# In segment 3 all transposes to tokens on VectorE; other places for mLSTM's chunks and for segment 0's inverse products

## The chip, the cores and the metric

One core of one Trainium2 chip. The metric is the device time of one execution in microseconds; lower is better. Engines are named as the profile names them: PE is TensorE (matmuls and transposes against an identity), DVE is VectorE, ACT is ScalarE, POOL is GpSimd, SP issues DMAs.

## What is computed

A decoder layer for 2048 tokens of width 1024 in float32. One input projection feeds two groups of heads: 4 heads of an mLSTM (key 128, value 256) and 8 heads of a gated DeltaNet (GDN; key and value 128). Both run in chunks with a state carried from chunk to chunk; one output projection follows. Of the reference, what matters here:

```python
# mLSTM, per chunk
num = (w_inter[..., None] * jnp.einsum('bhld,bhde->bhle', qi, C)
       + jnp.einsum('bhls,bhse->bhle', P, vi))
C = decay[..., None, None] * C + jnp.einsum('bhs,bhsd,bhse->bhde', ws, ki, vi)
...
# GDN: the inverse of a unit lower triangular matrix, then the chain of chunks
a_mat = lower + jnp.eye(CHUNK, dtype=lower.dtype)
sol = lax.linalg.triangular_solve(a_mat, rhs, left_side=True, lower=True, unit_diagonal=True)
...
v_new = Ui - jnp.einsum('bhld,bhde->bhle', Wi, S)
S = (jnp.exp(g_last)[..., None, None] * S
     + jnp.einsum('bhld,bhle->bhde', ki * jnp.exp(g_last[..., None] - gi)[..., None], v_new))
```

## The kernel before

The tokens are cut into 4 segments of 512, each with 4 chunks of 128. A segment is a row of windows: P0 M0 P1 M1 P2 M2 P3 M3, in the last segment P0 M0 P1 M1 P2 P3 M2 M3. A P window projects q, k, v and the gate of one pair of GDN heads (with a short convolution on DVE, L703 and L709); an M window projects one mLSTM head. The projection's matmuls fill the window, and `window()` (L1026) mixes other work between them, the streams: each stream is a generator, and a list of places (shares of the window's length, or a start, an end and a number of even steps between them) says when it makes its next step. The code is run on PE in the order in which it is written (`manual_schedule` for PE); the order of the instructions on DVE, ACT, POOL and SP is set by a scheduler when the kernel is built, with priorities as hints. Each engine executes its own list strictly in order.

Names are built as kind, segment, pair or head, chunk: `vr3_1_3` belongs to segment 3, pair 1, chunk 3. The streams, and the names that the prediction uses:

- `g_prep` of a pair: its k, q and v become "token-major" (`ktok`, `gv`), products of keys `kk` on PE, `ua` from them on DVE (L835), and then the **substitution**: 62 small DVE operations in a strict chain, 31 times L853 and L857 on `xb`/`tb`, with the columns shrinking from 31 blocks of 8 to 1. Its result goes to DRAM and back (`e_d`, L859; `E`, L863, four DMAs that SP issues).
- `g_level` of a pair: three DVE transposes turn `E` into `dmz` (L907, L908, L907), and four products on PE combine the small inverses: `zp` (L913), `fp` (L922), `zq` (L933), `fq` (L939). Between zp and fp ACT copies `dmz` from PSUM (L917), between fp and zq ACT writes `E` (L926) and DVE transposes it (L928).
- `g_chain` of a pair: four chunks, each `vp` (the transposes of v, when PE does them, L957), `sp`, `vr` on DVE (L979), `vq` (L985), a copy on ACT, `su`, `op`, the states `SS` on DVE (L1009), and the gated output `gyt` (L1021).
- `m_chunks` of a head: four chunks, each `nd` and `up` (L620, or L623 to L625 in split form), then on DVE the state `CN` (L651, L653) and the output `yt` (L670). In segment 0 the keys are weighted into `kws` by ACT (L612) and DVE (L613), four pieces in turn.

A block of 128x128 can be turned to tokens in two ways, by table, for each segment class (first, middle, last) and each pair or head: by PE against an identity (L957 for v, L773 for k, L876 for q, L602 for mLSTM's k), four instructions for 128x512; or by DVE, sixteen instructions of 32x128 (L504, in `to_tokens`), and for q by a reduction that transposes (L871, L888, L890). `VT`, `KTR`, `QT`, `MT` are the tables. In the middle segments (1 and 2) all of it is on DVE already. For q, k and v of a pair, an entry 1 means DVE.

After segment 3 comes a tail with the output projection, 16 tiles.

Of the kernel before, what the change touches and what calls it, by code (L numbers as in the profile page):

```python
# [26 lines left out]
XKB = 2  # L27
PRI = 400

LVP = (0.26, 0.3, 0.34, 0.4, 0.45)  # L30


CHP = (0.42, 0.46, 0.63, 0.71, 0.88)
CHM = (0.03, 0.11, 0.28, 0.45, 0.53, 0.7, 0.87, 0.95)
MW, MPR, VPR = ((0.07, 0.85), 200, 200)
MCP = (0.6, 0.75, 0.875)
MC2 = (0.0, 0.1, 0.18, 0.25, 0.32)
RMSP = (0.2, 0.22, 0.55, 0.55)
# [14 lines left out]
GN = 2  # L53


VT = ((0, 0, 0, 0), (1, 1, 1, 1), (1, 0, 0, 0))
KTR = ((0, 0, 0, 0), (1, 1, 1, 1), (0, 1, 0, 0))
QT = ((1, 1, 1, 1), (1, 1, 1, 1), (1, 1, 0, 1))
MT = ((0, 0, 0, 0), (1, 1, 1, 1), (1, 1, 1, 0))
KF = ((0, 1, 1, 1), (1, 1, 1, 1), (1, 1, 1, 0))  # L60
MF = ((1, 1, 1, 0), (1, 1, 1, 0), (1, 0, 0, 0))
KE = ('vector', 'gpsimd')
# [7 lines left out]
def hybrid_layer(  # L70
# [872 lines left out]
    def g_chain(seg, pr, r, st):  # L943
# [7 lines left out]
        def tok(c):  # L951
            n_ = f"{s_}_{c}"
            vr = sm.tile([P, 2, P], F32, tag="vr", name=f"vr{n_}", bufs=2)
            if not by_dve(VT, seg, pr):
                vp = psc.tile([P, 512], F32, tag="cp", name=f"vp{n_}")
# [146 lines left out]
    lvl, chain, mch = {}, {}, {}  # L1102
    st = None
    for seg in range(NSEG):
        last = seg == NSEG - 1
        pst, st = st, {}
        if seg:
            with tc.high_priority(PRI):
                build_h(pst["xks"])
        raw[0] = seg == 0  # L1110
        gs = gate_steps(seg, st)

        def nextrms():
            yield
            d = rms_stats(seg + 1)
            yield
            rbc = wkp.tile([P, T], F32, tag="gbc", name=f"rbc{seg + 1}", bufs=2)
            rms_bcast(seg + 1, d, rbc)
            yield
            st["xks"] = load_h(seg + 1, rbc)  # L1120

        for kind, n in ORDER_LAST if last else ORDER:
            r = {}
            streams, keep = [], ()
            if kind == "P":
                q = 3 if n == 0 else n - 1
                if n == 0 and seg:
                    streams.append((mch.pop(3), MC2, None, None, 2 * PRI))
                if n == 0:
                    streams.append((gs, GP, None, None, PRI))  # L1130
                    if seg == 0:
                        streams.append((rms_first_bcast(), (RB,), None, None, PRI))
                if last and n == 3:
                    streams.append((prep2, 10, 0.0, 0.2, PRI))
                    if LVB[0] < 0:
                        streams.append((lvl[2], NLV, 1 + LVB[0], 1 + LVB[1], PRI))
                elif last and n == 2:
                    streams += [(lvl[q], LVA[0], None, None, PRI), (chain[q], NCS, LVA[1], LVA[2], PRI),
                                (mch[q], 8, MW[0], MW[1], MPR)]
                elif q in chain:  # L1140
                    streams += [(lvl[q], LVP, None, None, PRI), (chain[q], CHP, None, None, PRI)]
                    if q in mch:
                        streams.append((mch[q], 8, MW[0], MW[1], MPR))
                    keep = (chain[q],)
                window(g_proj(seg, n, r, st), WIN, streams, keep)
                lvl[n], chain[n] = g_level(seg, n, r), g_chain(seg, n, r, st)
                prep = g_prep(seg, n, r, st)
                if last and n == 2:
                    prep2 = prep
            else:  # L1150
                if last and n == 2:
                    if LVB[0] >= 0:
                        streams.append((lvl[2], NLV, LVB[0], LVB[1], PRI))
                    streams += [(prep, 10, 0.0, 0.25, PRI), (chain[2], NCS, LVB[2], LVB[3], PRI)]
                    if LVC[0] < 0:
                        streams.append((lvl[3], NLV, 1 + LVC[0], 1 + LVC[1], PRI))
                elif last and n == 3:
                    if LVC[0] >= 0:
                        streams.append((lvl[3], NLV, LVC[0], LVC[1], PRI))
                    streams += [(mch[2], 8, LVC[4], LVC[5], PRI),  # L1160
                                (chain[3], NCS, LVC[2], LVC[3], PRI)]
                else:
                    streams.append((prep, 10, 0.0, 0.25, PRI))
                    if (n - 1) % 4 in chain:
                        streams.append((chain[(n - 1) % 4], CHM, None, None, PRI))
                mch[n] = m_chunks(seg, n, r, st)
                if n == 3:
                    if last:
                        streams.append((wout_early(), WOP, None, None, 0))
                    else:  # L1170
                        streams.append((nextrms(), RMSP, None, None, 0))
                    streams.append((mch[n], MCL if last else MCP, None, None, 0))
                    keep = (mch[n],)
                window(m_proj(seg, n, r), WIN, streams, keep)
# [232 lines left out]
```

## Time and profile before

| what | value |
|---|---|
| time, median of 3 runs | 2287.14 us (2284.95 to 2287.39) |
| the profiled execution | 2287.61 us |
| its span | 2285.8 us, 41796 instructions |
| granted PE clock, mean | 0.988 |
| busy PE, DVE, ACT, POOL | 2204.7, 1829.0, 861.3, 804.4 us |
| segment 0 (first to last window) | 7 to 485 us |
| segments 1, 2 and 3 | 485 to 956, 956 to 1420, 1420 to 1905 us |
| tail | 1905 to 2286 us |

The profile gives for one execution the busy time of each engine, what ended its idle time (a wait is put down to the instruction that came last), and a timeline of instructions. Granted clock 1.00 is 2.4 GHz and 0.50 is 1.2 GHz. Times inside the profile count from the span's start; 1.8 us of the profiled execution lie around the span.

### The profile page before, as it was taken

The page shows a single profiled execution, that of the slowest core. Times are in us where ns is not written, and L with a number is a line of the kernel's source. Part 1 is how long each engine was busy: PE and PEld are TensorE (multiplying, and loading weights), DVE is VectorE, ACT ScalarE, POOL GpSimd, SP SyncE. Part 2 cuts the span into 40 slices and gives each one's busy share as a digit, 9 for nine tenths or more (in the row PEclk, how much of TensorE's full clock was granted, in tenths as well). Part 3 has the DMA queues.
Part 4 walks back from the last instruction along what each step waited for, and adds up shares of the span by engine and source line. Part 5 has one row for each costly group of instructions (what it writes and reads, how often), then busy time and mean ns, then how long its engine had stood idle before and what let it go on. Part 6 is the DMA issues. An engine that isn't in the chain of part 4 may idle for free.

```text
span 2285.8 us, 41796 instructions
## 1 busy us (share of the span) xinstructions
PE 2204.7 (96%) x14814; PEld 1956.3 (86%) x14814; DVE 1829.0 (80%) x5108; ACT 861.3 (38%) x2289; POOL 804.4 (35%) x1219
## 2 busy tenths in 40 slices
PE   8989999989999999999999999999999999999998
PEld 7869898987989898978898989798988997788777
DVE  8978878778997979889979798698767737878784
ACT  5535454535343434352424243434244334111111
POOL 5747565652121202521212124212111115555543
PEclk9999999999999999999999999999999999999999
DMA  8767767764636364655454547454546544222321
GB/s 288 265 213 243 246 225 244 263 223 138 213 129 210 138 218 150 233 167 182 158 192 160 187 162 239 154 172 167 183 166 208 188 158 162 80 97 91 102 83 65
DMA packets 183322, 409.19 MB, mean 179 GB/s; under 512 B 51736, under 2 KB 84632, under 8 KB 183112
## 3 DMA queue, kind: packets, MB, share of 16 engines
q1 hardware_dynamic: 182392, 405.74, 52.4%
q8 instruction: 116, 1.90, 0.3%
q14 instruction: 94, 0.77, 0.1%
q10 hardware_dynamic: 720, 0.79, 0.1%
HBM read 309.68 MB, written 96.90 MB: 178 GB/s over the span
## 4 chain that ended last, share of the span: by engine, by line
PE 53%; DVE 27%; POOL 4%; DMA 4%; issue 4%; ACT 3%; SPq 0%; POOLq 0%; ACTq 0%; DVEq 0%
DVE ytt L1222 5%; DVE ktok L504 3%; PE pt_gz L365 2%; PE pt_gz L363 2%; PE pt_gz L364 2%; PE po L1263 2%; PE po L1262 2%; PE po L1261 2%; DVE gv L504 2%; PE pt_mv L363 2%; PE pt_mo L365 2%; PE pt_mo L363 2%; PE pt_mo L364 2%; PE pt_mv L365 2%; PE pt_mv L364 2%
## 5 line engine op out<-in xcount | busy, mean ns | idle before, releaser
L1222 DVE STREAM_TRANSPOSE ytt<-yl 32x256 f32<-32x256 f32 x448 | 195.3, 436 | 45.3 <-POOL ylo L1190 39.2
L1019 POOL TENSOR_TENSOR gms<-gms,nhalf 128x2 f32<-128x2 f32 x64 | 49.8, 779 | 401.2 <-DVE gms L1017 400.9
L853 DVE TENSOR_TENSOR tb<-xb,lbt 128x248 f32<-128x248 f32 (+30 forms) x496 | 167.1, 337 | 28.8 <-DMA lbt<-l_d 16.2
L857 DVE TENSOR_TENSOR xb<-xb,tb 128x248 f32<-128x248 f32 (+30 forms) x496 | 167.6, 338 | 13.1
L363 PE MATMUL pt_gz<-whi_P,hh 128*128 128x256 f32 (+1 forms) x512 | 151.2, 295 | 4.8 <-ACT hh L341 3.4
L365 PE MATMUL pt_gz<-whi_P,hl 128*128 128x256 f32 (+1 forms) x512 | 147.6, 288 | 2.4 <-DVE hl L342 2.4
L364 PE MATMUL pt_gz<-wlo_P,hh 128*128 128x256 f32 (+1 forms) x512 | 147.6, 288 | 1.8 <-DVE wlo_P L182 1.8
L363 PE MATMUL pt_mo<-whi_M,hh 128*128 128x256 f32 x512 | 148.3, 290 | 0.0
L363 PE MATMUL pt_mz<-whi_M,hh 128*128 128x256 f32 x512 | 147.7, 288 | 0.0
L363 PE MATMUL pt_mv<-whi_M,hh 128*128 128x256 f32 x512 | 147.0, 287 | 0.0
L365 PE MATMUL pt_mo<-whi_M,hl 128*128 128x256 f32 x512 | 144.2, 282 | 0.0
L365 PE MATMUL pt_mz<-whi_M,hl 128*128 128x256 f32 x512 | 144.1, 281 | 0.0
L364 PE MATMUL pt_mv<-wlo_M,hh 128*128 128x256 f32 x512 | 144.1, 281 | 0.0
L365 PE MATMUL pt_mv<-whi_M,hl 128*128 128x256 f32 x512 | 144.0, 281 | 0.0
L364 PE MATMUL pt_mo<-wlo_M,hh 128*128 128x256 f32 x512 | 144.0, 281 | 0.0
L364 PE MATMUL pt_mz<-wlo_M,hh 128*128 128x256 f32 x512 | 144.0, 281 | 0.0
L1270 ACT ACTIVATE jkf<-xr 128x512 f32<-128x512 f32 (+1 forms) x33 | 20.4, 619 | 271.8 <-DVE xr L1268 148.1
L1261 PE MATMUL po<-woh,yh 128*128 128x512 f32 (+1 forms) x297 | 114.6, 386 | 1.7 <-ACT yh L1188 1.7
L1262 PE MATMUL po<-wol,yh 128*128 128x512 f32 (+1 forms) x297 | 114.4, 385 | 0.9 <-POOL wol L1068 0.9
L1263 PE MATMUL po<-woh,ylo 128*128 128x512 f32 (+1 forms) x297 | 114.7, 386 | 0.1
L182 POOL TENSOR_TENSOR wlo_M<-wraw_M,whi_M 128x256 fp32r<-128x256 f32 x128 | 99.8, 811 | 40.5 <-ACT whi_M L179 40.2
L182 POOL TENSOR_TENSOR wlo_P<-wraw_P,whi_P 128x256 fp32r<-128x256 f32 x104 | 87.9, 874 | 62.9 <-ACT whi_P L179 58.1
(409 smaller groups left out, 7543.5 us busy)
## 6 DMA issues: line engine op xcount, KB each, us to landing
whi_M<-wdM SPq DMA_DIRECT2D x96, 512.0 KB, 3.8
wlo_M<-wdM SPq DMA_DIRECT2D x96, 512.0 KB, 5.1
whi_P<-wdP SPq DMA_DIRECT2D x90, 512.0 KB, 4.1
wlo_P<-wdP SPq DMA_DIRECT2D x90, 512.0 KB, 5.6
wraw_M<-in_wg_dram SPq DMA_DIRECT2D x32, 512.0 KB, 6.6
wdM<-whi_M SPq DMA_DIRECT2D x32, 512.0 KB, 2.7
wdM<-wlo_M SPq DMA_DIRECT2D x32, 512.0 KB, 3.0
wraw_P<-in_wg_dram SPq DMA_DIRECT2D x30, 512.0 KB, 7.2
```

The source lines that it names most:

```text
L182: eng.tensor_tensor(lo[:, ks, :], raw_[:, ks, :], hi[:, ks, :].bitcast(F32), op=ALU.subtract)
L363: nc.tensor.matmul(ps, lhsT=hh[k][:, ts], rhs=hi, start=(k == 0), stop=False)
L364: nc.tensor.matmul(ps, lhsT=hh[k][:, ts], rhs=lo, start=False, stop=False)
L365: nc.tensor.matmul(ps, lhsT=hl[k][:, ts], rhs=hi, start=False, stop=(k == KT - 1))
L504: nc.vector.transpose(dst[32 * a:32 * a + 32, :, 32 * b:32 * b + 32], s4[32 * b:32 * b + 32, :, a, :])
L853: nc.vector.tensor_tensor(tb[:, :, 0:n], xb[:, :, i:i + 1].broadcast_to([P, 8, n]), lbt[:, i:i + 1, i + 1:32].broadcast_to([P, 8, n]), op= ...
L857: nc.vector.tensor_tensor(xs, xs, tb[:, :, 0:n], op=ALU.subtract)
L1019: nc.gpsimd.tensor_tensor(ms, ms, nhalf[:, 0:2], op=ALU.pow)
L1222: nc.vector.transpose(ytt[32 * b:32 * b + 32, :, 32 * a:32 * a + 32], y3[32 * a:32 * a + 32, :, 32 * b:32 * b + 32])
L1261: nc.tensor.matmul(ps, lhsT=yh, rhs=woh, start=(k == 0), stop=False)
L1262: nc.tensor.matmul(ps, lhsT=yh, rhs=wol, start=False, stop=False)
L1263: nc.tensor.matmul(ps, lhsT=ylo, rhs=woh, start=False, stop=(k == 15))
```

## The change

Three edits. The last row of the four tables becomes all 1: in segment 3 every transpose to tokens is on DVE. `MW`, a start and an end for eight even places (two steps a chunk, so 0.07, 0.181, 0.293, 0.404, 0.516, 0.627, 0.739, 0.85), becomes a written list of eight. In segment 0 the inverse products of a pair get the places `LV0` in the next pair's window.

```diff
-LVP = (0.26, 0.3, 0.34, 0.4, 0.45)
+LVP, LV0 = (0.26, 0.3, 0.34, 0.4, 0.45), (0.33, 0.37, 0.42, 0.48, 0.53)
...
-MW, MPR, VPR = ((0.07, 0.85), 200, 200)
+MW, MPR, VPR = ((0.07, 0.18, 0.29, 0.4, 0.51, 0.6, 0.79, 0.86), 200, 200)
...
-VT = ((0, 0, 0, 0), (1, 1, 1, 1), (1, 0, 0, 0))
-KTR = ((0, 0, 0, 0), (1, 1, 1, 1), (0, 1, 0, 0))
-QT = ((1, 1, 1, 1), (1, 1, 1, 1), (1, 1, 0, 1))
-MT = ((0, 0, 0, 0), (1, 1, 1, 1), (1, 1, 1, 0))
+VT = ((0, 0, 0, 0), (1, 1, 1, 1), (1, 1, 1, 1))
+KTR = ((0, 0, 0, 0), (1, 1, 1, 1), (1, 1, 1, 1))
+QT = ((1, 1, 1, 1), (1, 1, 1, 1), (1, 1, 1, 1))
+MT = ((0, 0, 0, 0), (1, 1, 1, 1), (1, 1, 1, 1))
...
                 elif last and n == 2:
                     streams += [(lvl[q], LVA[0], None, None, PRI), (chain[q], NCS, LVA[1], LVA[2], PRI),
-                                (mch[q], 8, MW[0], MW[1], MPR)]
+                                (mch[q], MW, None, None, MPR)]
                 elif q in chain:
-                    streams += [(lvl[q], LVP, None, None, PRI), (chain[q], CHP, None, None, PRI)]
+                    streams += [(lvl[q], LVP if seg else LV0, None, None, PRI), (chain[q], CHP, None, None, PRI)]
                     if q in mch:
-                        streams.append((mch[q], 8, MW[0], MW[1], MPR))
+                        streams.append((mch[q], MW, None, None, MPR))
```

Line numbers of the changed kernel are one higher from L34 on (L504 before is L505 after). How the lists of the engines move is shown at three places.

DVE in segment 1, P1, where chunk 2 of mLSTM's head 0 ends (`yt1_0_2`), before:

```order
1112 L709 SCALAR_TENSOR_TENSOR xingv1_1_0_7844<-xingv1_1_0_7844,gv1_1_0_7787 128x512
1113 L666 TENSOR_SCALAR mr21_0_2_7899<-mr21_0_2_7899 128x1
1114 L504 STREAM_TRANSPOSE gv1_1_0_7787<-xingv1_1_0_7844 32x4x32 x8
1115 L1009 SCALAR_TENSOR_TENSOR SS0_251<-SS0_251,egl1_6683,su1_0_0_7931 128x128
1116 L504 STREAM_TRANSPOSE gv1_1_0_7787<-xingv1_1_0_7844 32x4x32 x4
1117 L670 SCALAR_TENSOR_TENSOR yt1_0_2_7892<-nd1_0_2_7875,mr21_0_2_7899,mg1_0_6731 128x256
1118 L1009 SCALAR_TENSOR_TENSOR SS1_252<-SS1_252,egl1_6683,su1_0_0_7931 128x128
1119 L504 STREAM_TRANSPOSE gv1_1_0_7787<-xingv1_1_0_7844 32x4x32 x4
1120 L1017 SCALAR_TENSOR_TENSOR gms1_0_0_7941<-gms1_0_0_7941,cq41_0_7006 128x2
```

and with the change:

```order
1110 L667 TENSOR_SCALAR mr21_0_2_7865<-mr21_0_2_7865 128x1
1111 L704 SCALAR_TENSOR_TENSOR gv1_1_0_7787<-xingv1_1_0_7875,conv_c_211,gv1_1_0_7787 128x512 x2
1112 L671 SCALAR_TENSOR_TENSOR yt1_0_2_7858<-nd1_0_2_7841,mr21_0_2_7865,mg1_0_6731 128x256
1113 L710 SCALAR_TENSOR_TENSOR xingv1_1_0_7875<-xingv1_1_0_7875,gv1_1_0_7787 128x512
1114 L1010 SCALAR_TENSOR_TENSOR SS0_251<-SS0_251,egl1_6683,su1_0_0_7931 128x128
1115 L1010 SCALAR_TENSOR_TENSOR SS1_252<-SS1_252,egl1_6683,su1_0_0_7931 128x128
1116 L505 STREAM_TRANSPOSE gv1_1_0_7787<-xingv1_1_0_7875 32x4x32 x11
1117 L1018 SCALAR_TENSOR_TENSOR gms1_0_0_7941<-gms1_0_0_7941,cq41_0_7006 128x2
1118 L505 STREAM_TRANSPOSE gv1_1_0_7787<-xingv1_1_0_7875 32x4x32 x5
```

`yt1_0_2` stood behind 12 of the 16 transposes of `gv1_1_0`; now it stands ahead of all 16. On PE `up1_0_3`, the last chunk's update, waits for `yt1_0_2`; it now stands 18 matmuls later. The same holds for P1 to P3 of segments 1 and 2.

DVE in segment 3, M2, where the last of pair 3's products of keys (`kk3_3_1_1`) goes into `ua3_3` and `dmz` of pair 2 is made. Before (the 62 substitution operations of pair 2 all stand ahead of these rows):

```order
3142 L835 SCALAR_TENSOR_TENSOR ua3_3_21564<-kk3_3_0_1_21641,scol3_3_21620,ua3_3_21564 128x256 x2
3143 L871 TENSOR_REDUCE qs3_3_21756<-qtp3_3_0_21757 128x16
3144 L907 STREAM_TRANSPOSE dmz_245<-E0_241 32x8x32
3145 L908 STREAM_TRANSPOSE dmz_245<-E0_241 32x8x32
3146 L907 STREAM_TRANSPOSE dmz_245<-E0_241 32x8x32
3147 L835 SCALAR_TENSOR_TENSOR ua3_3_21564<-kk3_3_1_0_21652,scol3_3_21620,ua3_3_21564 128x256 x2
3148 L871 TENSOR_REDUCE qs3_3_21756<-qtp3_3_1_21791 128x16
3149 L835 SCALAR_TENSOR_TENSOR ua3_3_21564<-kk3_3_1_1_21665,scol3_3_21620,ua3_3_21564 128x256 x2
```

and with the change:

```order
3141 L836 SCALAR_TENSOR_TENSOR ua3_3_21721<-kk3_3_1_0_21797,scol3_3_21765,ua3_3_21721 128x256 x2
3142 L858 TENSOR_TENSOR xb3_2_21100<-xb3_2_21100,tb3_2_21253 128x8x21
3143 L854 TENSOR_TENSOR tb3_2_21253<-xb3_2_21100,lbt3_2_21244 128x8x20
3144 L858 TENSOR_TENSOR xb3_2_21100<-xb3_2_21100,tb3_2_21253 128x8x20
3145 L836 SCALAR_TENSOR_TENSOR ua3_3_21721<-kk3_3_1_1_21810,scol3_3_21765,ua3_3_21721 128x256 x2
3146 L854 TENSOR_TENSOR tb3_2_21253<-xb3_2_21100,lbt3_2_21244 128x8x19
3147 L858 TENSOR_TENSOR xb3_2_21100<-xb3_2_21100,tb3_2_21253 128x8x19
```

```order
3182 L854 TENSOR_TENSOR tb3_2_21253<-xb3_2_21100,lbt3_2_21244 128x8
3183 L858 TENSOR_TENSOR xb3_2_21100<-xb3_2_21100,tb3_2_21253 128x8
3184 L908 STREAM_TRANSPOSE dmz_245<-E0_241 32x8x32
3185 L909 STREAM_TRANSPOSE dmz_245<-E0_241 32x8x32
3186 L908 STREAM_TRANSPOSE dmz_245<-E0_241 32x8x32
```

Between the two pieces shown there are only substitution operations of pair 2: 38 of its 62 now stand behind L836 of `kk3_3_1_1`, and `dmz` behind them. The 64 transposes of `ktok3_3` and `gv3_3`, which PE did before, stand ahead of the first piece, mixed with the first 24. On PE, `zp3_2` is the next work that is no projection behind `kk3_3_1_1`, as before.

ACT in segment 0, P1, between the level products of pair 0 and the keys of mLSTM's head 0, before:

```order
107 L700 ACTIVATE gk0_1_1_1523<-xingk0_1_1_1576,conv_c_211 128x512
108 L612 ACTIVATE kws0_0_pt_1627<-ktp0_0_1622,ws0_757 128x128 x2
109 L917 COPY dmz_245<-zp0_0_1643 32x8x32 x2
110 L612 ACTIVATE kws0_0_pt_1627<-ktp0_0_1622,ws0_757 128x128
111 L707 ACTIVATE xingk0_1_1_1576<-gk0_1_1_1523 128x512
112 L612 ACTIVATE kws0_0_pt_1627<-ktp0_0_1622,ws0_757 128x128
113 L926 ACTIVATE E0_241<-fp0_0_1668 32x8x32 x2
114 L700 ACTIVATE gq0_1_0_1611<-xingq0_1_0_1694,conv_c_211 128x512
```

and with the change:

```order
107 L701 ACTIVATE gk0_1_1_1523<-xingk0_1_1_1576,conv_c_211 128x512
108 L613 ACTIVATE kws0_0_pt_1627<-ktp0_0_1622,ws0_757 128x128 x3
109 L708 ACTIVATE xingk0_1_1_1576<-gk0_1_1_1523 128x512
110 L613 ACTIVATE kws0_0_pt_1627<-ktp0_0_1622,ws0_757 128x128
111 L918 COPY dmz_245<-zp0_0_1665 32x8x32 x2
112 L701 ACTIVATE gq0_1_0_1611<-xingq0_1_0_1652,conv_c_211 128x512
113 L658 ACTIVATE yt0_0_0_1702,mss0_0_0_1701<-nd0_0_0_1692 128x256
114 L640 CAST cn0_0_1_tb_1813<-CN0_247 128x258
115 L927 ACTIVATE E0_241<-fp0_0_1719 32x8x32 x2
```

The copies of `dmz` from `zp0_0` (L917, now L918), for which `fp0_0` waits, stood between the second and the third piece of `kws0_0`; now they stand behind the fourth. On PE the products stand 12 (zp) to 27 (fq) rows later than before, and `nd0_0_0` and `up0_0_0` now stand between zp and fp; before they stood behind zq. `vq0_0_0` keeps its row. Pairs 1 and 2 of segment 0 move in the same way.

## Rows read from the trace of the kernel before

**Rows 1.** The page, part 1: busy time, share of the span and instructions of each engine.

```profile
PE 2204.7 (96%) x14814; PEld 1956.3 (86%) x14814; DVE 1829.0 (80%) x5108; ACT 861.3 (38%) x2289; POOL 804.4 (35%) x1219
```

**Rows 2.** Waits of PE, whole span. Columns: engine, line, waited for, us in total, times, longest.

```profile
PE up L623 <- DVE yt L670: 10.8, 6, 2.3
PE fp L922 <- ACT dmz L917: 5.6, 3, 3.1
PE zq L933 <- DVE dmz L928: 5.1, 4, 1.6
PE zp L913 <- DVE dmz L907: 4.3, 2, 2.6
```

**Rows 3.** Windows P2 and P3 of segment 3: stretch and length, busy us, granted clock, DMA.

```profile
1658.29:1722.40 64.11, 64.11 (x453) 55.84 (x452) 35.75 (x95) 26.08 (x71) 11.84 (x29) 1.00 0.47 157
1722.23:1771.83 49.60, 49.60 (x283) 43.12 (x282) 40.52 (x110) 21.99 (x67) 10.05 (x16) 1.00 0.69 230
```

**Rows 4.** Lines of PE, 1420 to 1925 us: count, busy us, mean ns, idle before.

```profile
L957 PE MATMUL vp<-ident,gv 128*128 128x128 f32 x24 | 4.6, 272 | 0.0
```

**Rows 5.** Lines of DVE, same stretch: the transposes to tokens that stand there already, and L871.

```profile
L504 DVE STREAM_TRANSPOSE gv<-xingv 32x128 f32<-32x128 f32 x32 | 9.7, 302 | 0.5
...
L871 DVE TRANSPOSE_TENSOR_REDUCE qs<-qtp 128x16 f32<-128x512 f32 x6 | 4.1, 702 | 0.0
```

**Rows 6.** Timeline, segment 1, P1: start us, length us, engine, line [idle before <- what ended it].

```profile
658.16 1.25 DVE L504 STREAM_TRANSPOSE gv<-xingv 32x128 f32<-32x128 f32 x4
...
659.45 0.48 DVE L670 SCALAR_TENSOR_TENSOR yt<-nd,mr,mg 128x256 f32<-128x256 f32 x1
...
659.99 0.39 PE L623 MATMUL up<-mv,kws_pt 128*128 128x258 f32 x1 [2.19 <-DVE yt L670]
```

**Rows 7.** Windows: P1 of segment 1 behind that wait; P1 of segment 0 at two clocks.

```profile
660.40:664.00 3.60, 3.60 (x20) 3.60 (x20) 3.53 (x10) 0.20 (x1) 2.43 (x4) 0.53 0.39 142
132.90:135.70 2.80, 2.80 (x14) 2.26 (x13) 1.28 (x2) 0.72 (x1) 0.19 (x1) 1.00 1.02 311
152.00:155.00 3.00, 3.00 (x9) 2.18 (x7) 1.10 (x2) 0.72 (x1) 0.19 (x1) 0.50 0.09 36
```

**Rows 8.** Timeline, segment 0, P1: the first products of pair 0 and what precedes them.

```profile
147.43 0.34 DVE L613 SCALAR_TENSOR_TENSOR kws_nm<-ktp,ws,kws_pt 128x128 fp32r<-128x128 f32 x1
...
148.20 0.75 ACT L917 COPY dmz<-zp 32x256 f32<-32x256 f32 x2
...
148.61 1.45 PE L922 MATMUL fp<-E,dmz 32*32 32x32 f32 x32 [3.07 <-ACT dmz L917]
...
150.19 0.35 ACT L612 ACTIVATE kws_pt<-ktp,ws 128x128 fp32r<-128x128 f32 x1
```

**Rows 9.** Timeline, segment 3, the end of P2 and the start of P3.

```profile
1716.83 0.61 DVE L979 SCALAR_TENSOR_TENSOR vr<-sp,neg,vr 128x128 f32<-128x128 f32 x2 [0.27 <-PE sp L976]
...
1718.41 0.60 PE L985 MATMUL vq<-vr,E 128*128 128x128 f32 x4
...
1726.59 0.28 PE L824 MATMUL kk<-kh 128*128 128x256 f32 x1
```

**Rows 10.** Windows: from pair 2's first L835 to its last substitution step.

```profile
1727.90:1777.60 49.70, 49.70 (x285) 43.19 (x284) 42.71 (x125) 21.96 (x65) 9.44 (x16) 1.00 0.69 231
```

**Rows 11.** Lines of DVE, 1763.5 to 1777.5 us: the last substitution steps of pair 2.

```profile
L857 DVE TENSOR_TENSOR xb<-xb,tb 128x144 f32<-128x144 f32 (+17 forms) x18 | 4.3, 236 | 0.4
L853 DVE TENSOR_TENSOR tb<-xb,lbt 128x144 f32<-128x144 f32 (+17 forms) x18 | 4.2, 236 | 0.5
```

**Rows 12.** Timeline, segment 3, M2: from the last substitution step of pair 2 to its first product.

```profile
1777.31 0.17 DVE L857 TENSOR_TENSOR xb<-xb,tb 128x8 f32<-128x8 f32 x1
...
1782.39 0.44 DVE L907 STREAM_TRANSPOSE dmz<-E 32x256 f32<-32x256 f32 x1
...
1783.52 0.39 PE L831 MATMUL kk<-gq,gk 128*128 128x128 f32 x2
...
1785.23 0.69 PE L913 MATMUL zp<-dmz,ua 32*32 32x32 f32 x32
```

## The prediction

> **What bounds the kernel now.** I read the busy times first: PE works 96% of the span, DVE 80%, the others under 40% [rows 1]. So the time is PE's work plus PE's waits, and the second view is the list of those waits [rows 2]. The reader is to see there that the largest is one pattern, six waits of `up` for `yt`, 10.8 us in sum, and that the next three are the small inverse products fp, zq and zp. The third view is the windows of segment 3, where the tables change: PE never idles in P2 and P3, and DVE is busy 35.7 of 64.1 us in P2 but 40.5 of 49.6 us in P3 [rows 3]. DVE's room, 28 us, then 9 us, is what the moved transposes have to fit into. The last view is the timeline at each place where PE waits or would wait [rows 6, 8, 9, 12], read together with the order of DVE's list.
>
> **MW.** At 659.99 us PE waits 2.19 us for a `yt` that DVE reaches only behind transposes, four of which take 1.25 us, so 0.31 each [rows 6]. In the list of the change this `yt` stands ahead of all 16: 12 transposes, 3.7 us, are gone from in front of it, more than the longest of the six waits (2.3), and `up` itself asks for it 18 matmuls later. All that stood between moves back by the 0.48 us of `yt` alone. The six waits go: -10.8. Behind the first of them the granted clock is 0.53, that is mostly 1.2 GHz, for 3.6 us [rows 7]; at full clock that work takes 1.9, so another 1.7 comes back. What is late next is chunks 1 and 2, which come a little earlier in PE's list and need a state from DVE. I take -12, with -4 (two thirds of the waits come back there) and -12.5 as ends.
>
> **LV0.** The targets are zp (4.3, both waits in pair 0) and fp (5.6: 3.07 in pair 0, 2.5 in pairs 1 and 2) [rows 2, 8], one of the four waits of zq, and the slow stretches behind them (clock 0.50 over the 3 us from 152 us on [rows 7]). It looks like 11 us and more. But fp waits for ACT's copies, L917, 0.75 us [rows 8], and these now stand behind all four pieces of `kws`, not two. A piece on ACT needs the piece before it finished on DVE; the fourth began at 150.19 with the copies ahead of it [rows 8], and the two convolutions and the L707 between the pieces set that, so it stays near 150.3. Copies and then fp come at about 151.1, not at 148.61: 2.5 us later, with 21 rows of PE more ahead of fp: 15 projection matmuls at 0.20 to 0.23 us (14 touch 2.8 us at full clock [rows 7]) and the six smaller ones of `nd0_0_0` and `up0_0_0`, about 4 us in sum. And `up0_0_0` now waits for the first DVE piece, which ends at 147.8 [rows 8]. Pair 0 is so about 1.5 us ahead at fp; a shorter slow stretch gives about as much again. In pairs 1 and 2 the same copies go behind the same four pieces, and their waits were smaller: nil. I take -3; ends -14 (the waits and half of the slow stretches go) and +3 (fp waits longer in each pair).
>
> **The tables, PE's side.** 60 transposes leave PE: 24 of v [rows 4], and 24 of k, 8 of q and 4 of mLSTM's k in the same shape. Four instructions of this shape take 0.60 us, the last of them 0.27 [rows 4, 9], so 0.11 each: -6.5 us, of which 20 (2.2 us) come after the place that decides below.
>
> **The tables, DVE's side.** Every four of the 52 for v and k become 16 instructions of 32x128 at 302 ns [rows 5], 0.31 with the gap [rows 6]: 208 of them, 65 us. Up to M1 segment 3 now has the lists of segment 2, and I take -1 there. In P2 the DVE has room, but not where it counts. `vr3_1_3` waits 0.27 us for PE and then runs, and its product on PE starts about a us behind it [rows 9]. Now 15 transposes of `gv3_2_1` (4.7 us) and three outputs (1.5 us) stand directly ahead of it: about 4.5 us of wait. Earlier, 32 transposes of `ktok3_2` and 16 of `gv3_2_0` make `vr` of chunks 0, 1 and 2 late by 0.3 to 1 us each: about 2.5. PE leaves P2 some 7 us late (ends 0 and 9).
>
> Then the place that decides. The substitution of pair 2 is DVE's longest chain, and `zp3_2` on PE waits for its end, the trip through DRAM, and three transposes. Before: last step from 1777.31, `dmz` done at 1782.83, zp at 1785.23, 2.4 us to spare [rows 12]. From the first L835 of pair 2 to the last step DVE is busy 42.7 of 49.7 us [rows 10], so 7 us of room. Now that stretch also holds the 64 transposes of pair 3 (20 us), and about 4 us more: two L871 (0.70 each [rows 5]) with their small copies, and four further L835 of pair 3, counted like `yt` at 0.48 [rows 6]; the eight scalings of pair 2's keys move out ahead of it. That is 67 us without any idle time. It begins when `kk3_2` is there, 1726.6 + 1.3 before [rows 9], now 1 + 0.9 earlier (transposes gone) and 7 later, at 1733. So the last step ends at 1800, and with the same 5.3 us for the trip and `dmz` zp can start at 1805: **20 us later than before**.
>
> A second way gives the same size. In DVE's list 38 substitution steps stand behind the L836 of `kk3_3_1_1`. The last 36 of before took 4.3 + 4.2 us [rows 11], so 38 take 9.1, and 10 with gaps. `zp3_2` is 1.3 us behind `kk3_3_1_1` on PE [rows 12]. Whatever happens earlier, PE must wait 0.5 + 10 + 5.3 - 1.3, about 14.5 us, there. With the 4.4 us that PE has saved by then the place is at least 10 us later than before.
>
> What follows the wait: -2.2 us of transposes; about +1.7 us of slow clock, at the price of [rows 7]. Substitution and products of pair 3 begin earlier relative to PE than before, so nothing more is late, and the tail is PE's own work and gives nothing back. Segment 3 in sum: 20 - 2.2 + 1.7, about **+20** (ends +8, from the second way with nothing late in P2, and +27, with 9 us in P2 and a longer trip).
>
> The Trainium skill, "VectorE: DVE Perf Modes", in "The three transpose paths", gives 311 ns for a 128x128 bf16 transpose on VectorE and 390 ns on TensorE. The trace here disagrees: 302 ns buys a quarter of a 128x128 block in float32.
>
> **The sum.** -12 - 3 + 20 = +5 on the profiled execution's 2287.6: 2292.6. That execution lies 0.5 above the median of the runs, so 2292 for a median. What a measurement of this kernel can tell from no change is about 0.2%, 4.6 us: the forecast stands just at that bound.
>
> **Rivals.**
> *LV0 does what it looks like.* If the pieces of `kws` come earlier, so that the copies behind them end before 148.6, fp waits no more: -14 in place of -3, the sum is -6, **2281**, faster. For it: PE sits idle for 3.07 us there [rows 8], so a wait that ends a little sooner is gained in full. Against: the chain of pieces is a ping-pong of two engines, and nothing in it is removed. 0.12.
> *P2 is not late.* DVE has 28 us of room there [rows 3]; if the scheduler's list runs smoother than I worked it, the deciding place begins at 1726 and segment 3 costs +12 to +13: sum -3, **2284**, no change. 0.17.
> *DVE has room after all.* If a whole 128x128 block cost DVE one instruction's 0.31 us, the 64 would be 5 us, the wait 15 us shorter, the sum -10, **2277**, faster. 32 instructions at 302 ns in [rows 5] speak against it. 0.06. By the figure of the Trainium skill, "VectorE: DVE Perf Modes", "The three transpose paths", the 64 would be 16 x 0.311 = 5 us, as an estimate, and the sum this rival's.
> *The wait of `up` comes back.* If chunks 1 and 2, now earlier, wait for the state from DVE, MW gives -4: sum +13, **2300**. For it: DVE is busy over 90% in these windows' second half, 3.53 of 3.6 us in the piece shown [rows 7]. Against: these places move by a matmul or two. 0.13.
>
> **How the numbers follow.** The forecast has 0.52, with a range of its own from 2287 to 2299; about two thirds of it lies above 2291.7. Slower by over 0.2%: 0.33 + 0.13 = 0.46. Within 0.2%: 0.18 of the forecast and nearly all of the second rival, 0.34. Faster: the first and the third and the rest, 0.20. The range of 8 in 10 leaves out the third rival and what lies beyond the fourth: 2278 to 2303.
>
> **What would show it.** Right: the wait of `up` for `yt` is gone from PE's list; a wait of zp for `dmz` (L908) of 12 us or more stands in M2 of segment 3, near 1790 to 1805; `vq` waits for `vr` at the end of P2; fp still waits for L918 in segment 0, and a wait of `up0_0_0` for `kws` is new; DVE is busy without a gap from P3 to that zp. Wrong: no wait of over 5 us in segment 3, or segment 0 shorter by over 8 us, or the waits of `up` replaced by ones of `nd` for the state.

## The result and the profile after

| | before | after |
|---|---|---|
| time, median | 2287.26 us | 2303.45 us (2302.31 to 2305.22, 4 runs) |
| profiled execution, span | 2287.61, 2285.8 us | 2302.31, 2300.5 us |
| granted PE clock, mean | 0.988 | 0.981 |

The ratio after to before is 1.0072, with a 95% interval of 1.0054 to 1.0089: slower, by 16 us. The direction was forecast; the size, +5 us, was not, and 2303.45 lies just above the range.

Busy times after, to be held against [rows 1]:

```profile
PE 2204.6 (96%) x14754; PEld 1954.2 (85%) x14754; DVE 1885.8 (82%) x5321; ACT 856.8 (37%) x2269; POOL 813.2 (35%) x1220
```

PE does 60 instructions fewer, and yet its busy time is the same to 0.1 us, at a mean granted clock of 0.981 instead of 0.988. DVE has 213 instructions and 57 us more. Then PE's waits, for [rows 2]:

```profile
PE zp L914 <- DVE dmz L908: 24.1, 3, 21.9
PE fp L923 <- ACT dmz L918: 6.7, 3, 2.4
PE zq L934 <- DVE dmz L929: 5.0, 4, 2.2
PE vq L986 <- DVE vr L980: 4.4, 2, 4.1
...
PE up L626 <- DVE kws_nm L614: 1.8, 3, 0.8
PE up L624 <- ACT kws_pt L613: 1.8, 1, 1.8
```

The 10.8 us of `up` for `yt` are gone without a successor. A single wait of `zp` is 21.9 us, the waits of `vq` for `vr` now stand in segment 3 (before, 2.8 us of them stood in segment 0), and two kinds of small waits of `up` for `kws` are new.

To see where the time went I took the same matmul of the projections in both traces and subtracted its start before from its start after. At 485 us of before's time (start of segment 1) the changed kernel is 2.3 us ahead, at 1420 (start of segment 3) 14.7 ahead, at 1706 (in P2) 13.0 ahead, at 1722 (start of P3) 5.0, at 1780 (in front of `zp3_2`) 7.8, and at 1789, behind it, 17.1 us **behind**; then 15 us behind to the end. So: segment 0 -2.3, segments 1 and 2 -12.4, segment 3 +29.6. The losses stand at two places, 8.0 us at the end of P2 and 24.9 at `zp3_2`.

The end of P2 after, on DVE and PE ([rows 9] before):

```profile
1704.33 4.74 DVE L505 STREAM_TRANSPOSE gv<-xingv 32x128 f32<-32x128 f32 x15
1709.10 0.42 DVE L732 SCALAR_TENSOR_TENSOR gg<-gtz,pt_gz 128x256 f32<-128x256 f32 x1
1709.43 0.60 DVE L1022 SCALAR_TENSOR_TENSOR gyt<-op,gms,gg 128x128 f32<-128x128 f32 x2
1709.95 0.47 DVE L671 SCALAR_TENSOR_TENSOR yt<-nd,mr,mg 128x256 f32<-128x256 f32 x1
1710.35 0.60 DVE L980 SCALAR_TENSOR_TENSOR vr<-sp,neg,vr 128x128 f32<-128x128 f32 x2
```

```profile
1710.74 1.22 PE L986 MATMUL vq<-vr,E 128*128 128x128 f32 x4 [4.05 <-DVE vr L980]
```

The 15 transposes and three outputs stand in front of `vr3_1_3` as the list said, and PE waits 4.05 us.

The deciding place, first the whole stretch from the first L836 of pair 2 to the last substitution step, then its three parts (columns as in [rows 3]: stretch, length, busy PE, PEld, DVE, ACT, POOL, clock):

```profile
1721.59:1794.23 72.64, 55.96 (x314) 48.42 (x312) 69.05 (x206) 21.61 (x52) 13.22 (x21) 0.91 0.53 178
...
1721.59:1741.08 19.49, 19.49 (x94) 16.24 (x93) 18.10 (x53) 9.58 (x22) 4.02 (x8) 1.00 0.80 256
1741.08:1783.76 42.68, 36.47 (x221) 32.18 (x219) 41.76 (x118) 12.03 (x32) 9.20 (x13) 0.97 0.52 183
1783.76:1794.30 10.54, 0.00 (x0) 0.00 (x0) 9.20 (x39) 0.00 (x0) 0.00 (x0) 0.50 0.09 14
```

DVE is busy 69 of 72.6 us where it was busy 42.7 of 49.7 [rows 10]. In the last row DVE does the 38 substitution steps, PE nothing at all, and the granted clock is 0.50, 1.2 GHz. The end of the chain and the product that waits for it ([rows 12] before):

```profile
1794.06 0.17 DVE L858 TENSOR_TENSOR xb<-xb,tb 128x8 f32<-128x8 f32 x1
1798.88 0.43 DVE L908 STREAM_TRANSPOSE dmz<-E 32x256 f32<-32x256 f32 x1 [4.64 <-DMA E<-e_d]
```

```profile
1799.45 0.28 PE L914 MATMUL zp<-dmz,ua 32*32 32x32 f32 x2 [21.90 <-DVE dmz L908]
1800.30 1.06 PE L914 MATMUL zp<-dmz,ua 32*32 32x32 f32 x30 [0.56 <-DVE dmz L908]
```

PE's last matmul in front of it ended at 1777.55; from there DVE needs 16.7 us more for the chain, the trip through DRAM takes 4.6 us, and the other two transposes of `dmz` hold the rest of the product back once more.

### The profile page after: what moved, and what is told of

Same layout as the page of the kernel before. It is cut to its first block, busy times and chain, and to the rows that moved or that the text cites. A ratio compares the mean times of both kernels' runs of the same rounds, so it can differ in the third digit from the quotient of the medians.

```text
span 2300.5 us, 41845 instructions
## 1 busy us (share of the span) xinstructions
PE 2204.6 (96%) x14754; PEld 1954.2 (85%) x14754; DVE 1885.8 (82%) x5321; ACT 856.8 (37%) x2269; POOL 813.2 (35%) x1220
## 4 chain that ended last, share of the span: by engine, by line
PE 59%; DVE 30%; DMA 4%; ACT 3%; issue 2%; POOL 1%; SPq 1%; POOLq 0%; DVEq 0%; ACTq 0%
PE po L1264 5%; PE po L1263 5%; PE po L1262 5%; DVE ktok L505 3%; DVE xb L858 3%; DVE tb L854 3%; DVE gv L505 3%; PE pt_mv L364 2%; PE pt_mo L365 2%; PE pt_gz L366 2%; PE pt_mo L364 2%; PE pt_mo L366 2%; PE pt_mv L366 2%; PE pt_mv L365 2%; PE pt_gz L364 2%
## 5 line engine op out<-in xcount | busy, mean ns | idle before, releaser
L858 DVE TENSOR_TENSOR xb<-xb,tb 128x248 f32<-128x248 f32 (+30 forms) x496 | 167.3, 337 | 13.2
L505 DVE STREAM_TRANSPOSE gv<-xingv 32x128 f32<-32x128 f32 x384 | 116.2, 303 | 5.7
L505 DVE STREAM_TRANSPOSE ktok<-gk 32x128 f32<-32x128 f32 x384 | 116.2, 303 | 5.5
```

What stands on the lines that cost most here:

```text
L505: nc.vector.transpose(dst[32 * a:32 * a + 32, :, 32 * b:32 * b + 32], s4[32 * b:32 * b + 32, :, a, :])
L858: nc.vector.tensor_tensor(xs, xs, tb[:, :, 0:n], op=ALU.subtract)
```

## The experiments

The theory: MW gives 12 us, LV0 next to nothing, and the tables cost 30 because `zp3_2` waits for a substitution that stands behind the transposes of pair 3, while P2 is late by pair 2's. The main rivals: that LV0 is worth its waits, that the tables are harmless without the other two edits, that pair 2's transposes (P2) and not pair 3's are the price.

### The three edits apart

Run e1_old_tables: the change with the four table rows of before.

```diff
-VT = (..., (1, 1, 1, 1))
+VT = (..., (1, 0, 0, 0))
-KTR = (..., (1, 1, 1, 1))
+KTR = (..., (0, 1, 0, 0))
-QT = (..., (1, 1, 1, 1))
+QT = (..., (1, 1, 0, 1))
-MT = (..., (1, 1, 1, 1))
+MT = (..., (1, 1, 1, 0))
```

> The change without its tables (MW and LV0 alone). Theory A, the two edits of places gain what segments 0 to 2 show in the trace (14.4 us at the start of segment 3, of them 2.3 in segment 0) and the tables alone lose: 2287.2 - 14.4 = 2272.8 us, segment 3 as before with no wait of zp. Theory B, part of the loss comes from the places (chunks of mLSTM closer together in segment 3): 2280 us or more.

Measured 2272.0 us, ratio 0.9935 [0.9917, 0.9953]. Two of the three edits, then, are a gain of 15 us.

Run e2_tables_alone: the kernel before with the four new rows, the reverse of that diff.

> Before, with the four last rows of the tables all 1 and nothing else. Theory A: segment 3 loses the same 28 us as in the change, and P1 of segment 3 gets a wait of up for yt like those of segments 1 and 2 (about 2 us): 2316 us. Theory B (the loss needs the new places too): under 2308 us.

Measured 2311.3 us, ratio 1.0109 [1.0074, 1.0144], between the two theories. The tables alone cost 25 us. The further wait of `up` for `yt` that was expected in segment 3 is not there (six waits and 10.8 us, as before). The wait of zp is that of the change:

```profile
1811.76 0.28 PE L913 MATMUL zp<-dmz,ua 32*32 32x32 f32 x2 [21.84 <-DVE dmz L907]
```

On top of the other two edits the tables cost 31 us (1.0072 less 0.9935). The intervals do not tell 25 from 31; in the trace 2.7 us of the difference lie at the end of P2 (+5.3 here, +8.0 in the change).

Run e8_mw_alone: before, with the list of eight places.

```diff
-MW, MPR, VPR = ((0.07, 0.85), 200, 200)
+MW, MPR, VPR = ((0.07, 0.18, 0.29, 0.4, 0.51, 0.6, 0.79, 0.86), 200, 200)
...
-                                (mch[q], 8, MW[0], MW[1], MPR)]
+                                (mch[q], MW, None, None, MPR)]
```

> Before, with the list of places MW alone. Theory A: the six waits of up for yt (10.8 us) and the slow clock behind the first (1.7) go: 2274.6 us. Theory B (they return in part as waits of nd for the state): 2279 us or more.

Measured 2275.8 us, ratio 0.9946 [0.9927, 0.9966], 12.4 us by the ratio: MW is worth what was forecast, and nothing of it comes back.

Run e7_lv0_alone: before, with the five places of segment 0.

```diff
-LVP = (0.26, 0.3, 0.34, 0.4, 0.45)
+LVP, LV0 = (0.26, 0.3, 0.34, 0.4, 0.45), (0.33, 0.37, 0.42, 0.48, 0.53)
...
-                    streams += [(lvl[q], LVP, None, None, PRI), ...]
+                    streams += [(lvl[q], LVP if seg else LV0, None, None, PRI), ...]
```

> Before, with LV0 in segment 0 and the old even places of MW. Theory A: fp waits behind the four pieces of kws instead, 2 to 3 us gained: 2284.5 us. Theory B (the waits that LV0 aims at are gained in full): 2276 us.

Measured 2288.3 us, ratio 1.0008 [0.9998, 1.0019]. LV0 gives nothing that can be measured; both theories here were too hopeful. Its waits in segment 0, P1, pair 0 ([rows 8] before):

```profile
148.19 0.39 PE L624 MATMUL up<-mv,kws_pt 128*128 128x258 f32 x1 [1.83 <-ACT kws_pt L613]
149.10 0.39 PE L626 MATMUL up<-mv,kws_nm 128*128 128x258 f32 x1 [0.41 <-DVE kws_nm L614]
152.85 1.06 PE L923 MATMUL fp<-E,dmz 32*32 32x32 f32 x32 [2.67 <-ACT dmz L918]
```

The 3.07 us in front of `fp` have become 1.83, 0.41 and 2.67: the copies do stand behind four pieces of `kws`, and the new waits of `up` take what the wait of `zp` gave (4.3 us in sum before, 1.5 with LV0 alone).

### Which transposes: pair 3's or pair 2's

Run e3_pair3_on_pe: the change, with k and v of pair 3 on PE.

```diff
-VT = (..., (1, 1, 1, 1))
-KTR = (..., (1, 1, 1, 1))
+VT = (..., (1, 1, 1, 0))
+KTR = (..., (1, 1, 1, 0))
```

> The change with k and v of pair 3 back on PE in segment 3: 64 of the 208 added transposes leave DVE, 16 return to PE. Theory A, DVE's order decides: these 64 stand ahead of the substitution of pair 2, so the wait of zp (22.5 us) and the slow clock behind it (about 1.8) go, 16 x 0.11 = 1.8 us come back on PE, and the lateness at the end of P2 stays: about 2281 us. Theory B, DVE's load decides and each transpose costs alike: 64/208 of 28 us: about 2295 us.

Measured 2278.7 us, ratio 0.9966 [0.9955, 0.9978]. In the list of waits from P2 to `zp3_2` one row alone is left:

```profile
PE vq L986 <- DVE vr L980: 4.0, 1, 4.0
```

The 64 transposes of pair 3, 19.4 us of DVE, make some 24 us of the change's time (1.0072 less 0.9966).

Run e9_pair2_on_pe: the same for pair 2.

```diff
-VT = (..., (1, 1, 1, 1))
-KTR = (..., (1, 1, 1, 1))
+VT = (..., (1, 1, 0, 1))
+KTR = (..., (1, 1, 0, 1))
```

> The change with k and v of pair 2 back on PE in segment 3. Theory A (two places, added up): PE leaves P2 in time (8 us less), 16 x 0.11 = 1.8 us come back on PE, and the wait of zp for the substitution of pair 2 stays at 20 us or more, since 43 of its steps (38 in the change) stand behind the last keys' product: 2297 us. Theory B (PE waits for DVE's sum at zp anyway, so what is late in P2 is hidden in that wait): 2303 us, with a wait of zp of about 30 us.

Measured 2297.5 us, ratio 1.0042 [1.0028, 1.0056], as expected. P2 is no longer late (offset from before the same at 1706 and 1722 us, to 0.1), yet the wait of zp is longer than in the change, 25.2 us: PE only comes to it sooner, and gives back at zp some 3 of the 8 us that it saves in P2. So pair 2's transposes make P2 late, by 7 to 8 us in each of the runs that have them there beside the new places (e3, e6, e13, e14) and by 5.3 with the old ones (e2), and pair 3's make the wait. By the ratios the two prices are 7 us (1.0072 less 1.0042) and 24, which add up to the 31 of the tables.

### Same work, another place

Run e6_defer_v: all transposes stay on DVE, but those of pair 3's v are made in the chain of chunks (into the ring of `ktok`, free by then), which puts them behind `zp3_2`. The part of the edit that leaves them out of the convolution's loop is not shown.

```diff
...
+        if seg == NSEG - 1 and pr == 3 and by_dve(VT, seg, pr):
+            for j in range(2):
+                t_ = wkp.tile([P, NCH, P], F32, tag=f"ktok{j}", name=f"gvt{s_}_{j}", bufs=2)
+                to_tokens(vT[j], t_)
+                vT[j] = t_
```

> The change with the same transposes on DVE, but the 32 of pair 3's v are made only when pair 2's keys are free, behind zp3_2 instead of ahead of it; 21 substitution steps stay behind the last keys' product instead of 38. Theory A (order): the wait of zp becomes shorter by the 10 us of these transposes, the rest as in the change: 2293 us. Theory B (load; DVE has the same work in all): 2303 us.

Measured 2298.1 us, ratio 1.0048 [1.0033, 1.0063], between the two numbers. The wait falls by what was expected, from 21.9 us to this:

```profile
1788.81 0.28 PE L915 MATMUL zp<-dmz,ua 32*32 32x32 f32 x2 [12.81 <-DVE dmz L909]
```

but behind it, where the change shows only a `zq` of 0.8 us up to 1850, new waits stand:

```profile
PE vq L992 <- DVE vr L986: 2.5, 1, 2.5
PE sp L983 <- DVE SS L1016: 1.5, 1, 1.5
```

The 32 transposes make the chain of chunks late instead. Nine microseconds out of the wait became some five in the time (1.0072 less 1.0048): the place where the work goes has less than 10 us of room for it.

### Pairs 0 and 1, and q of pair 2

Run e5_pairs01: the change with k and v of pairs 2 and 3 on PE. Of the tables there remain v of pair 1, k of pair 0, q of pair 2 and mLSTM's k.

```diff
-VT = (..., (1, 1, 1, 1))
-KTR = (..., (1, 1, 1, 1))
+VT = (..., (1, 1, 0, 0))
+KTR = (..., (1, 1, 0, 0))
```

> The change with k and v of pairs 2 and 3 on PE in segment 3; on DVE stay, beyond the kernel before, k of pair 0, v of pair 1, q of pair 2 and k of mLSTM's head 3. Theory A (only transposes of the two windows next to the last substitutions cost, the others are hidden): 28 x 0.11 = 3.1 us of PE less than in the run with the old tables (2272.0): 2269 us. Theory B (each transpose on DVE costs): 80 of 208 of 28 us more: 2280 us.

Measured 2285.2 us, ratio 0.9985 [0.9973, 0.9998]: a miss for both theories. A wait of 8.4 us at `zp3_2` is still there. The substitution of pair 2 on DVE, first in e1:

```profile
1727.45 0.41 DVE L854 TENSOR_TENSOR tb<-xb,lbt 128x248 f32<-128x248 f32 x1
...
1761.34 0.17 DVE L858 TENSOR_TENSOR xb<-xb,tb 128x8 f32<-128x8 f32 x1
```

then in e5:

```profile
1733.69 0.42 DVE L854 TENSOR_TENSOR tb<-xb,lbt 128x248 f32<-128x248 f32 x1 [2.01 <-DMA lbt<-l_d]
...
1763.75 3.42 DVE L963 TENSOR_SCALAR ktok<-ktok,ksc 128x128 f32<-128x128 f32 x7
1767.09 0.17 DVE L858 TENSOR_TENSOR xb<-xb,tb 128x24 f32<-128x24 f32 x1
...
1770.86 0.17 DVE L858 TENSOR_TENSOR xb<-xb,tb 128x8 f32<-128x8 f32 x1
...
1777.31 0.43 DVE L908 STREAM_TRANSPOSE dmz<-E 32x256 f32<-32x256 f32 x1 [5.49 <-DMA E<-e_d]
```

It starts 6.2 us later (1.0 of it is PE's own offset at the start of P3, -14.9 against -15.9) and ends 9.5 later. Six steps of 0.2 us, 1.2 us of work, have fallen behind the scalings and products of pair 3 and take 7.4 us, so the chain is 3.3 us longer than in e1. I had looked only for steps behind the last product of pair 3, of which there are none here. From the end of the last step to the first transpose of `dmz` it is 6.3 us, against 4.1 in e1. There `dmz` was ready 2.4 us before PE came to `zp3_2`. 6.2 + 3.3 + 2.2 - 2.4 is 9.3, and the two waits of zp in e5 are 9.0 us (8.4 and 0.6).

What stands in front of the first step and did not before is q of pair 2: two reductions L872 and seven small operations. But the first step also waits 2.0 us for `lbt`, the operand that is made of `ua` and goes through DRAM like `E`, as `l_d`. SP's queue (SPq: start and length of an issue) in e1, then in e5:

```profile
1717.47 1.80 SPq L845 DMA_DIRECT2D l_d<-ua  x4
...
1721.10 2.36 SPq L849 DMA_DIRECT2D lbt<-l_d  x4
```

```profile
1720.34 0.38 SPq L162 DMA_DIRECT2D whi_P<-wdP  x1
1720.82 0.38 SPq L162 DMA_DIRECT2D wlo_P<-wdP  x1
1721.29 2.63 SPq L845 DMA_DIRECT2D l_d<-ua  x4
...
1728.38 2.37 SPq L849 DMA_DIRECT2D lbt<-l_d  x4
```

In e5 two loads of weights (512 KB each) stand directly ahead of `l_d`, and from its issue to that of `lbt` it is 7.1 us, against 3.6 in e1. Two runs tell whether q is the cause of the wait, and two more whether it costs as much in other kernels.

Run e10_q_old: e5 with q of pair 2 on PE.

```diff
-QT = (..., (1, 1, 1, 1))
+QT = (..., (1, 1, 0, 1))
```

> Run e5 put k and v of pairs 0 and 1 and q of pair 2 on VectorE and came out at 2285.2 us, 13 us above run e1 (old tables, 2272.0), with a wait of 8.4 us at pair 2's first inverse product. This run is e5 with q of pair 2 left on TensorE (transposed there, squared by ScalarE). Theory A: q's two transposing reductions and seven small additions and copies of pair 2, which stand between the last product of pair 2 and the first substitution step, moved that step from 1727.45 us in e1 to 1733.69 us in e5, and with it the last six steps behind pair 3's key products. Then the wait of 8.4 us goes and the time is that of e1, at most 2 us less (16 transposes fewer on TensorE): 2269 to 2272 us. Theory B: the key and value transposes of pairs 0 and 1 make VectorE late: the wait stays, 2282 to 2286 us.

Run e12_q_alone: e1 with q of pair 2 on DVE, the reverse edit.

> Run e1 (old tables, 2272.0 us) with one entry of the four tables changed: q of pair 2 on VectorE. Theory A (q of pair 2 is what made e5 miss): the wait of about 8.4 us at pair 2's first inverse product is there, first substitution step about 6 us later than in e1, time 2280 to 2285 us. Theory B: no such wait, 2271 to 2273 us.

Measured: e10 2274.5 us, ratio 0.9945 [0.993, 0.996], 2.5 us above its forecast but not to be told from e1 by the intervals, and with no wait of PE from 1700 to 1800 us; e12 2288.6 us, ratio 1.0006 [0.9993, 1.0019], 3.6 us above its forecast, with the wait:

```profile
1780.23 0.28 PE L914 MATMUL zp<-dmz,ua 32*32 32x32 f32 x2 [8.25 <-DVE dmz L908]
```

One entry of a table, 2.6 us of DVE's work (two L872 of 0.70 and 1.2 for the small ones), costs 16 us between e1 and e12 and 9 between e10 and e5, by the ratios. That q of pair 2 is the cause is shown, in both directions. How it turns 2.6 us into 9 or more is shown in part: from the issue of `l_d` to that of `lbt` it is 7.5 us in e12, with two loads of weights directly ahead of `l_d` as in e5, and 3.2 in e10, without them. No run moves these loads alone, so their share stays open. The k of pair 0, the v of pair 1 and mLSTM's k cost nothing that can be told (e10 against e1), and the PE time that they free cannot be seen either.

Run e13_all_but_q: the change, with that one entry as before (the edit of e10).

> The change as it is (2303.5 us), with q of pair 2 alone left on TensorE. Theory A: q's reductions are one part of the VectorE stretch that ends with the last substitution step (2 of 0.71 us and seven small ones, about 2.8 us of busy time ahead of the first step; 33 instead of 38 steps stand behind pair 3's products), and the wait of 21.9 us shrinks by 3 to 9 us: 2294 to 2300 us. Theory B: q of pair 2 is hidden here behind other waits: 2302 to 2304 us, wait 21 to 22 us.

Measured 2306.9 us, ratio 1.0088 [1.0071, 1.0105], not faster than the change: theory B, if anything, and 2.9 us above it. The last step starts at 1790.14 instead of 1794.06 us, but 3.2 of these 3.9 us are PE's own offset in front of zp (-11.0 against -7.8). From the first L836 to the end of the last step it is 72.8 us, as in the change (72.6): DVE's work there falls from 69.05 to 68.02, and its idle time grows from 3.6 to 4.8. So the wait is 20.9 us, 1 us less; and the next wait takes that back, `zq` for `dmz`, 3.22 us where the change has 0.84:

```profile
1807.38 1.96 PE L934 MATMUL zq<-dmz,ua 64*64 64x64 f32 x16 [3.22 <-DVE dmz L929]
```

Run e14_p3_q2_on_pe: e3 with the same entry.

> Run e3 (the change with k and v of pair 3 on TensorE, 2278.65 us) with q of pair 2 on TensorE as well, so that pair 2's k and v and the m-chain's transposes alone are added to the old tables. In e3 no wait at pair 2's first inverse product was listed, and 4.0 us of the 6.6 us that it lies above e1 were the wait of vq at the end of P2. Theory A: q of pair 2 costs only where the inverse product waits: 2277 to 2280 us. Theory B: q of pair 2 costs VectorE time on the path here too: 2270 to 2275 us.

Measured 2276.9 us, ratio 0.9959 [0.9944, 0.9974], theory A. In e3 P2 is 7 us late, so PE comes that much later to `zp3_2`, and q is covered by it: the last transpose of `dmz` ends at 1778.90 us, `zp3_2` starts at 1779.24 without a wait. Taking q away has nothing to gain there.

The shifts of the same projection matmuls against before, in us, in the profiled executions of all these kernels, each the difference of the shifts at two places:

| run | segment 0 (to 485) | segments 1, 2 (485 to 1420) | end of P2 (1706 to 1722) | zp3_2 (1780 to 1789) |
|---|---|---|---|---|
| the change | -2.3 | -12.4 | +8.0 | +24.9 |
| e1 old tables | -2.3 | -12.8 | 0.0 | -0.1 |
| e2 tables alone | -1.2 | +3.2 | +5.3 | +24.3 |
| e7 LV0 alone | +0.1 | +1.5 | +0.1 | -0.1 |
| e8 MW alone | -2.4 | -11.3 | 0.0 | 0.0 |
| e3 pair 3 on PE | +2.1 | -10.5 | +7.1 | 0.0 |
| e9 pair 2 on PE | -0.4 | -13.0 | -0.1 | +27.9 |
| e6 v of pair 3 later | -0.6 | -12.4 | +7.7 | +16.4 |
| e5 pairs 0, 1 and q | +0.9 | -12.1 | -0.2 | +11.8 |
| e10 pairs 0, 1 | +0.3 | -8.2 | -0.1 | 0.0 |
| e12 q alone | +0.8 | -13.2 | 0.0 | +11.9 |
| e13 all but q | -0.8 | -12.4 | +7.1 | +23.6 |
| e14 pair 2 without q | -3.0 | -10.9 | +8.0 | 0.0 |

The first two columns say what one execution can tell: the ten kernels with both LV0 and MW differ in segment 3 alone, and they lie between -3.0 and +2.1 in segment 0 and between -8.2 and -13.2 in segments 1 and 2. The last two columns span a few microseconds each and scatter far less: where no wait stands they read -0.2 to +0.1. Of all these e1, at 2272 us, is the fastest and beats both kernels; e8, e10 and e14 follow within 5 us.

## Why the prediction was right in direction and too small

By its own steps:

- **MW, -12: right.** Measured -12.4 in the trace and -12.4 by the ratio of e8 (-11.3 in segments 1 and 2 of its trace). The waits of `up` for `yt` went as the list said, and no wait took their place; the rival in which they come back (2300 us) is out.
- **LV0, -3: nothing.** The mechanism, copies behind four pieces of `kws` and new waits of `up`, was as described; that pair 0 is still ahead was too hopeful. The -2.3 of the trace is inside the scatter of one execution, and e7 gives nothing. The rival of 2281 us is out.
- **P2, +7: right in size, in its largest part for the right reason, in the rest by luck.** Measured +8.0, with 4.05 of it in the one wait that was put at 4.5. Of the 2.5 us put on `vr` of chunks 0 to 2 the list has one wait of 0.35 us, and 0.9 of `sp` for a state; up to the large wait the shift grows by 1.1. The other 2.6 us stand behind that wait (the offset is -7.7 at `vq` and -5.0 at 1722), where the granted clock is 0.50, a term that the prediction had only behind `zp3_2`:

```profile
1711.00:1716.00 5.00, 5.00 (x24) 5.00 (x25) 0.89 (x5) 2.51 (x15) 1.65 (x1) 0.50 0.37 110
```

  The rival of 2284 us is out.
- **Up to M1, -1.** From 1420 to 1706 us the change lost 1.7 us where 1 was to be gained; e3, e9 and e13 gain 3 there and e6 1, with the same tables up to M1, so the 2.7 us of difference are within the scatter of one execution.
- **zp3_2: the step that failed, by the size of a term.** The prediction put the start of the stretch 5.1 us later than before, its length at "67 us without any idle time", and the trip at 5.3. Counted from the start of segment 3 (14.7 us added to times after), the first L836 stands at 1736.3, not 1733: 3.3 us, which is no error of its own but what the two items above bring along (1.7 where -1 was put, 8.0 where 7 was). The stretch is 72.6 us long, not 67: 5.6. From the last step's end to the second part of zp it is 6.1, not 5.3: 0.8. In sum 9.7, and segment 3 lost 29.6 instead of 20. So about two thirds of the miss, 6.4 us, were counted wrongly in the stretch and the trip; the rest came late to it.
- **Within the stretch** both halves of "67 without idle" failed. The work is 69.05, not 66.7 (42.7 + 20 + 4). From its lines after,

```profile
L505 DVE STREAM_TRANSPOSE ktok<-gk 32x128 f32<-32x128 f32 x32 | 9.7, 303 | 0.4
L505 DVE STREAM_TRANSPOSE gv<-xingv 32x128 f32<-32x128 f32 x32 | 9.7, 302 | 0.4
L836 DVE SCALAR_TENSOR_TENSOR ua<-kk,scol,ua 128x256 f32<-128x256 f32 x16 | 6.9, 473 | 1.9 <-PE kk L827 1.9
...
L872 DVE TRANSPOSE_TENSOR_REDUCE qs<-qtp 128x16 f32<-128x512 f32 x3 | 2.1, 708 | 0.1
L963 DVE TENSOR_SCALAR ktok<-ktok,ksc 128x128 f32<-128x128 f32 x8 | 1.9, 278 | 0.0
```

  the 64 transposes are 19.4 us as put, but L836 stands there 16 times, eight more than before (3.4 us then), and I had counted four more; a third L872 and the eight scalings of pair 3's keys I had not counted (those of pair 2, 1.7 of the 42.7 us, moved out). Once the chain's steps fall behind pair 3's products, all of pair 3's work of that stage is in the stretch. And the idle time is 3.6 us, not none: 1.4 us before the first step, 0.9 in the mixed part, 1.3 in the last 38 steps. The prediction had that last piece right in its second way ("9.1, and 10 with gaps") and then left it out of the first.
- **The second way** was a lower bound and held: 14.5 us against 22.5. It reached PE's wait only if DVE was at the heels of PE. The last `kk` product of pair 3 started at 1775.77 on PE, and DVE came to its L836 at 1782.97, 7 us behind. That is most of the difference of 8.
- **After the wait**: -2.2 us of transposes, as put (the offset falls from 17.1 to 14.9). The slow clock costs 2.0 (the offset is 15.1 at zp and 17.1 at 1789); 1.7 was put. Behind the wait the clock is 0.50, then 0.66:

```profile
1799.40:1803.00 3.60, 2.98 (x36) 2.53 (x37) 3.23 (x12) 0.73 (x2) 0.00 (x0) 0.50 0.32 77
1803.00:1806.00 3.00, 3.00 (x39) 2.07 (x38) 2.79 (x9) 0.58 (x1) 0.00 (x0) 0.66 0.00 0
```

- **The rival "DVE has room after all"** fell by the trace before and after: 302 and 303 ns buy 32x128, and some 24 us hang on it (e3). With it falls the estimate that the prediction made from the Trainium skill, "VectorE: DVE Perf Modes", "The three transpose paths", 5 us for the 64: measured 19.4. The page gives its 311 ns for a bf16 block, and no run here turns one. The prediction's word that the trace disagrees goes too far: the figure does not carry over to these float32 instructions of 32x128.

What the prediction did not see at all is that q of pair 2 alone is enough for a wait of 8 us (e12). In the full change taking it away gains nothing (e13). The sign that DVE would be busy without a gap from P3 to that zp did not come: 3.6 us of gaps in the stretch and 4.6 in the trip. The other signs of being right all came.

That the ends of segment 3 were put at +8 and +27 was the second mistake: the upper end allowed 9 us in P2 and a longer trip, but no error in the count of the stretch, the largest number of all.

## What to carry to other kernels

An engine with 20% of idle time may have no room where a strict chain of small operations on it releases the busiest engine. Read that room from the stretch between the chain's first input and its waiter, count every instruction that the new list puts between the two, look at where the chain's last steps stand (in e5 six of them, 1.2 us of work, took 7.4 us behind another stage's block), and at what the list of DMAs puts in front of the chain's own transfers. Price the edits of one change one by one: here one gave 12 us, one nothing, and one took 25 on its own and 31 beside the others, and the version without it (2272 us) is the best.

## What the runs showed of the hardware

- The steps of the strict chain do not overlap when they stand alone: 38 in 10.54 us for 9.20 us of busy time, about 35 ns between one and the next. The first 24 steps, mixed with other instructions, leave DVE idle for only 0.92 of 42.68 us.
- The trip from the last substitution step through DRAM to `dmz` leaves DVE idle for 4.39 to 4.64 us in the runs where `zp3_2` waits longest (the change, e6, e9, e13), and 5.25 and 5.49 us in e12 and e5; there it is 6.0 and 6.3 us from the step's end, with one product of pair 3 in between. In e12 and e5 two loads of weights stand between `e_d` and `E` on SP's queue, in the other four none does.
- The trip of `ua` to `lbt` goes the same way: from the issue of `l_d` to that of `lbt` it is 7.1 to 7.6 us in the runs with two loads of weights directly ahead of it (e5, e9, e12), and 3.2 to 4.0 without (e1, e3, e6, e10, e13, the change). That the loads are the reason was not tried by itself in either trip.
- PE at a granted clock of 0.50 after a wait was seen before [rows 7]. Behind waits of 2.19, 4.05 and 21.9 us it costs about 1.7 (the prediction's estimate), 2.6 and 2.0 us: the price does not grow with the wait.
